# Rotary embedding of queries and keys cut into eight steps and spread over the attention heads, with the weight granules paired and ordered anew

## The chip, the cores and the metric

The kernel runs as one program on one core of a Trainium2 chip. The metric is device time in microseconds from the program's start to its end. Engine names are those of the profile: PE is TensorE's matrix multiply, PEld its weight load, DVE is VectorE, ACT is ScalarE, POOL is GpSimd, SP is SyncE, which issues most DMAs.

## What is computed

One layer of a flow-matching trunk on 640 tokens (512 latent tokens and 128 prompt tokens), width 1024, all in float32: a gated feed-forward half step, a mixing stage, and a second half step. The mixing stage runs eight heads of differential attention beside four heads of an mLSTM memory. The part that the change touches is the head of the attention:

```python
dq = rmsnorm(dq.reshape(B, T, DA_HEADS, 2, DA_HEAD_DIM), p['g_qn'][l])
dk = rmsnorm(dk.reshape(B, T, DA_HEADS, 2, DA_HEAD_DIM), p['g_kn'][l])
...
q_att = rope_2d(dq)
keys = jnp.concatenate([rope_2d(dk), k_ctx.astype(dk.dtype)], axis=1)
...
s = jnp.einsum('bqhcd,bkhcd->bhcqk', qi, kf) * scale
pr = jax.nn.softmax(s, axis=-1)
w = pr[:, :, 0] - lam * pr[:, :, 1]
return jnp.einsum('bhqk,bkhv->bqhv', w, vf)
```

Queries and keys are normalised per group of 64 numbers and then rotated by position ("rope"); prompt tokens are scaled only. Products are made from float32 numbers split into a high and a low part (H and L in the names), three matmuls for each product.

## The kernel before

Matmuls are written in a fixed order by hand (`mm`, L75, and the transposes, L78). On the other engines a scheduler places an instruction where it thinks best, unless it is issued inside `written()`: then instructions of one engine keep the order in which the code issues them.

**The attention** is the loop over eight heads and, within a head, five query blocks (qi 0 to 3 see 768 keys, qi 4 is the prompt block with 128). For one block: `scores` (eight matmuls into a three-bank PSUM tile `sc` of which there is one, then on DVE `mn`, L1674, the row minimum), `soft` (two exponentials on ACT, `p<-sc,mn`), `mix` (on DVE `rc`, `r` and the sum `p<-p,r,p`, L57), and, in the next block's place on PE, `turn` (transposes `ps_wT<-ident,p`) and `values` (`ps_o<-v_tok,wT`, evicted by DVE as `ao`, L61). At a head's end `finish_norm` normalises `ao` on DVE and ACT, and `finish` transposes it (`ps_aT<-ident,ao`) early in the next head. The next head's queries and keys are split by `pack` at qi 3 and transposed (`ps_qkT`) at the head's end.

**Fill units.** Between these steps PE is given other work from a queue, `Fill`: products of weight granules with the tokens, in units. A narrow token granule (`token`, 256 columns) has 5 units of 24 matmuls; two granules taken together (`wide`, 512 columns, in a PSUM bank of their own, `wide_ps`) have 10 units of 12 matmuls; a `feature` granule has 4 units of 24. The table `UNITS` says how many units stand in each block: a pair (1, 1) is two, (1, 0) is one. A granule's weights are split on ACT (`wH`) and DVE (`wL`, 2048 numbers per partition). Keys and queries of head pair `pr` (two heads) come from `project_k(pr)` and `project_q(pr)`, values from `project_v(pr)`; `memory_values`, `queries_of_memory` and `keys_of_memory` serve the later memory stage. In one unit order, 102 units are queued, the same ones before and after the change.

**The rotation.** When the last unit of a query or key granule is evicted by ACT, `qk_norm_rope` is issued at once, outside `written()`: a square on ACT (`rope<-k_tok`, 1280 numbers per partition), a sum on DVE (`ss`), a reciprocal root of 20 numbers (Ln and Exp on ACT, Newton on DVE, names `rv`, `rt`, `ry`), the scaling of 1280 numbers, a swapped copy on ACT (`rope<-k_tok`, 1024 numbers), and four more passes on DVE (times sine, times cosine, sum, prompt block times its gain). The scheduler sets these among the other DVE work. For a wide pair of keys and queries both rotations start with the same unit.

**PSUM pools.** Before the attention, a pool of five banks (`ps2`) serves the gate products, whose last results are evicted as `g_out` (the tile `ps_f`). It is closed, and two pools take over its banks in the order of their opening: `ps2m` (four banks, tag "mm", for all small tiles and narrow units) and `ps2w` (one bank, for wide units). A new tile waits until what last stood in its bank is evicted.

Of the kernel before, what the change touches and what calls it, by code (L numbers as in the profile page):

```python
# [31 lines left out]
def tile_trunk(ctx: ExitStack, tc: tile.TileContext, a: dict):  # L32
# [1494 lines left out]

    at_rope = [None]

    def qk_norm_rope(raw, tab):  # L1530
        A, B, g = tab
        sq = rope_place("q")
        act(sq, raw, AF.Square)
        ss = rope_p[0].tile([128, 20], F32, tag="ss", name="ss", bufs=2)
        vec.tensor_reduce(out=ss, in_=sq.rearrange("p t (g d) -> p (t g) d", d=64), axis=AX.X, op=ALU.add)
        rs = rstd_of(rope_p[0], ss, 1.0 / 64, [128, 20], "qk")
        r3 = raw.rearrange("p t (g d) -> p (t g) d", d=64)
        tt(vec, r3, r3, rs[:, :, None].to_broadcast([128, 20, 64]), ALU.mult)
        sw = rope_place("k")[:, 0:4]
        at_rope[0] = act(  # L1540
            sw.rearrange("p t (b s j) -> p (t b) s j", s=2, j=16),
            raw[:, 0:4, :].rearrange("p t (b s j) -> p (t b) s j", s=2, j=16)[:, :, ::-1, :],
            AF.Copy,
        )
        s4 = sw.rearrange("p t (g d) -> p t g d", d=64)
        q4 = raw[:, 0:4, :].rearrange("p t (g d) -> p t g d", d=64)
        tt(vec, s4, s4, B[:, :, None, :].to_broadcast([128, 4, 4, 64]), ALU.mult)
        tt(vec, q4, q4, A[:, :, None, :].to_broadcast([128, 4, 4, 64]), ALU.mult)
        tt(vec, raw[:, 0:4, :], raw[:, 0:4, :], sw, ALU.add)
        p3 = raw[:, 4, :].rearrange("p (g d) -> p g d", d=64)  # L1550
        tt(vec, p3, p3, g[:, None, :].to_broadcast([128, 4, 64]), ALU.mult)

    q_tok, k_tok, v_tok = {}, {}, {}

    def project_q(pr, now=lambda f: f()):
        def make():
            q_tok[pr] = t = (ap if pr % 2 else qk).tile([128, 5, 256], F32, tag="qtok", name="q_tok")

            def evac(p, i):
                act(t[:, i, :], p, AF.Copy)  # L1560
                if i == 4:
                    now(lambda: qk_norm_rope(t, tabs[0]))

            return evac

        return a["w_dq"][pr], make

    def project_k(pr, now=lambda f: f()):
        def make():
            t = (ap if pr % 2 else qk).tile([128, 5, 256], F32, tag="ktok", name="k_tok")  # L1570
            k_tok[pr] = t

            def evac(p, i):
                act(t[:, i, :], p, AF.Copy)
                def whole():
                    qk_norm_rope(t, tabs[1])
                    nc.sync.dma_start(out=a["new_k"][:, pr * 256 : (pr + 1) * 256], in_=t[:, 4, :])

                if i == 4:
                    now(whole)  # L1580

            return evac

        return a["w_dk"][pr], make
# [237 lines left out]
    token(project_v(0))  # L1822
    token(project_k(1))
    token(project_q(1))
    wide(project_v(1), memory_values(0))
    projections(2)
    queries_of_memory(1)
    wide(project_v(2), memory_values(1))
    projections(3)
    wide(project_v(3), memory_values(2))  # L1830
    keys_of_memory(1)
    queries_of_memory(2)
    keys_of_memory(2)
    queries_of_memory(3)
    values_of(3)
    feature(a["w_mk"][3], last_keys)
    gate_unit(a["w_gm"], gm_dram, 3, memory)
    gate_unit(a["w_gd"], gd_dram, 3, memory)
# [157 lines left out]
    ada.close()  # L1996
    right.close()
    banks.close()
    psum = att.enter_context(tc.tile_pool(name="ps2m", bufs=4, space=PSUM, reuse_waits="tile"))
    wide_ps.append(att.enter_context(tc.tile_pool(name="ps2w", bufs=1, space=PSUM, reuse_waits="tile")))  # L2000
    ap = att.enter_context(tc.tile_pool(name="att", bufs=1, reuse_waits="tile"))
    rope_p[0] = ap
    gt = gates.enter_context(tc.tile_pool(name="gates", bufs=1))
# [30 lines left out]
    late = None  # L2034
    for hd in range(8):
        H = heads[hd]
        for qi in range(5):
            n = UNITS[hd][qi]
            with written():
                H.scores(qi)  # L2040
                if qi > 0:
                    H.turn(qi - 1)
                H.soft(qi)
            aside(hd, qi, 0)
            fill.units(n[0])
            with written():
                H.mix(qi)
            if late is not None:
                late()
                late = None  # L2050
            if qi > 0:
                with written():
                    H.values(qi - 1)
            if qi == 3 and hd < 7:
                with written():
                    heads[hd + 1].pack()
            aside(hd, qi, 1)
            if (hd, qi) == (0, 2):
                begin_pools()
            fill.units(n[1])  # L2060
            with written():
                fill.ahead()
        n = UNITS[hd][-1]
# [571 lines left out]
```

## Time and profile before

| | |
|---|---|
| three runs | 1815.42, 1811.67, 1814.11 us; median 1814.11 |
| the profiled execution | 1810.32 us, of which the span from first to last instruction is 1808.4 |
| PE, PEld, DVE, ACT busy | 98%, 95%, 74%, 50% of the span |
| granted TensorE clock | 1.0 of full speed |
| attention stage | from about 650 us (first fill unit) to about 1065 us of the span |

The page of the profile gives busy shares; the view by windows gives the busy time of every engine in a stretch; the view of waits names for each idle time of an engine the instruction that ended it; the timeline gives start, duration and, in brackets, the idle time before an instruction. A share of the page is an average over stages with different limits, so the stage of the change is read by itself. In the groups view the last columns are busy time in us and the mean of one instruction in ns.

### The profile page before, as it was taken

Reading aid. Unit: us, or ns where it says so; the run is one execution under the profiler, and the core shown is the slowest. Engines: PE = TensorE matmul, PEld = TensorE weight load, DVE = VectorE, ACT = ScalarE, POOL = GpSimd, SP = SyncE. Lnnn points to the kernel's source line nnn. Section 1 sums busy time; section 2 is a strip of 40 time slices with the busy share of each in tenths; the row PEclk is TensorE's granted clock in tenths of the full one; section 3 lists DMA queues with packets and bytes.
Section 4 is the critical chain, followed back from the end, with each engine's and each line's share of the span. In section 5 each row is a group of like instructions: output and inputs, shape, how many; then the busy total and the mean of one; then the engine's idle time right before and its main releaser. Section 6 shows DMA issues by size and latency. Waiting matters only on the chain.

```text
span 1808.4 us, 29656 instructions
## 1 busy us (share of the span) xinstructions
PE 1778.9 (98%) x11950; PEld 1713.3 (95%) x11950; DVE 1346.6 (74%) x2162; ACT 900.2 (50%) x1579; POOL 41.0 (2%) x72
## 2 busy tenths in 40 slices
PE   8999999999999999999999999999999999999998
PEld 7999999999999999898889998899999999999998
DVE  6889987677988768667586447877668888897475
ACT  5654544333655456554565447562326545554432
POOL 0000000100000000000000000000000000000010
PEclk9999999999999999999999999999999999999999
DMA  8355566978245533312223335665652455557992
GB/s 325 114 198 173 185 236 220 351 223 272 84 138 183 195 129 100 110 61 69 75 72 110 106 99 197 188 244 205 217 173 77 134 173 187 203 180 272 355 311 84
DMA packets 144923, 317.85 MB, mean 176 GB/s; under 512 B 10577, under 2 KB 106577, under 8 KB 133009
## 3 DMA queue, kind: packets, MB, share of 16 engines
q1 hardware_dynamic: 133410, 270.20, 43.9%
q0 software_dynamic: 10688, 43.13, 7.4%
q10 hardware_dynamic: 688, 2.63, 0.4%
q8 instruction: 94, 1.54, 0.3%
q14 instruction: 43, 0.35, 0.1%
HBM read 243.77 MB, written 72.15 MB: 175 GB/s over the span
## 4 chain that ended last, share of the span: by engine, by line
PE 84%; DVE 8%; DMA 5%; ACT 2%; issue 1%; SPq 0%; DVEq 0%; ACTq 0%
PE ps_f L75 48%; PE ps_p L75 14%; PE ps_t L75 11%; PE sc L75 3%; PE ps_o L75 2%; PE ps_n L75 2%; DVE ww L54 2%; DMA raw_a<-in_w_ada_k 1%; PE ps_wT L78 1%; DMA P<-nm_dram 1%; PE ps_u L75 1%; PE ps_qkT L78 1%; DVE junk L814 1%; DMA raw<-in_w2b 1%; DMA a_raw<-aT_dram 1%
## 5 line engine op out<-in xcount | busy, mean ns | idle before, releaser
L75 PE MATMUL ps_f<-S,ww 128*128 128x320 f32 x2400 | 387.0, 309 | 3.2 <-DMA S<-g_dram 1.0
L75 PEld LDWEIGHTS ps_f<-S,ww 128*128 128x128 f32 x2400 | 359.8, 188 | 7.2 <-DVE ww L54 4.6
L54 DVE TENSOR_TENSOR ww<-raw,ww 128x2048 fp32r<-128x2048 f32 (+1 forms) x73 | 163.9, 2245 | 65.5 <-ACT ww L51 65.4
L75 PE MATMUL ps_f<-hm,ww 128*128 128x320 f32 x1176 | 185.6, 309 | 0.1
L75 PEld LDWEIGHTS ps_f<-hm,ww 128*128 128x128 f32 x1176 | 175.7, 188 | 0.3 <-DVE ww L54 0.3
L51 ACT ACTIVATE ww<-raw 128x2048 fp32r<-128x2048 f32 (+1 forms) x73 | 136.8, 1875 | 57.1 <-DVE raw L54 37.8
L54 DVE TENSOR_TENSOR raw<-raw 128x1024 f32<-128x1024 f32 x186 | 160.7, 864 | 2.4
L75 PE MATMUL ps_f<-hm,wB 128*128 128x320 f32 x1008 | 161.5, 309 | 0.0
L75 PE MATMUL ps_t<-wH,hH 128*128 128x256 f32 (+1 forms) x440 | 151.4, 344 | 2.9 <-DVE g_out L54 1.5
L75 PE MATMUL ps_p<-hH,wH 128*128 128x320 f32 x480 | 151.1, 315 | 1.6 <-DVE num L54 1.4
L75 PEld LDWEIGHTS ps_f<-hm,wB 128*128 128x128 f32 x1008 | 151.3, 188 | 0.0
L75 PE MATMUL ps_p<-hH,wL 128*128 128x320 f32 x480 | 148.3, 309 | 0.0
L75 PE MATMUL ps_p<-hL,wH 128*128 128x320 f32 x480 | 148.3, 309 | 0.0
L75 PE MATMUL ps_t<-wH,hL 128*128 128x256 f32 (+1 forms) x440 | 146.7, 333 | 0.9 <-DVE hL L54 0.9
L75 PE MATMUL ps_t<-wL,hH 128*128 128x256 f32 (+1 forms) x440 | 146.2, 332 | 0.0
L51 ACT ACTIVATE u<-ps_f 128x320 f32<-128x320 f32 x129 | 55.8, 433 | 157.0 <-PE ps_f L75 156.9
L51 ACT ACTIVATE wH<-raw 128x2048 fp32r<-128x2048 f32 (+1 forms) x45 | 75.4, 1683 | 48.8 <-PE ps_p L75 37.3
L54 DVE TENSOR_TENSOR wL<-raw,wH 128x2048 fp32r<-128x2048 f32 x37 | 84.6, 2286 | 19.5 <-ACT wH L51 19.3
L1674 DVE TENSOR_REDUCE mn<-sc 128x2 f32<-128x1536 f32 (+1 forms) x40 | 59.6, 1490 | 50.2 <-PE sc L75 50.0
L54 DVE TENSOR_TENSOR wB<-raw,wB 128x1024 fp32r<-128x1024 f32 x64 | 78.0, 1219 | 24.4 <-ACT wB L51 24.4
L814 DVE CUSTOM_DVE_ANT_0 junk<-raw_a,csil 128x1024 bf16<-128x1024 f32 (+1 forms) x76 | 92.5, 1217 | 2.1 <-DMA raw_a<-in_w_ada_c 1.6
L75 PEld LDWEIGHTS ps_t<-wH,hH 128*128 128x128 f32 x440 | 83.6, 190 | 11.0 <-DVE g_out L54 1.7
(306 smaller groups left out, 3595.9 us busy)
## 6 DMA issues: line engine op xcount, KB each, us to landing
g_dram<-g SPq DMA_DIRECT2D x44, 640.0 KB, 7.6
raw_a<-in_w_ada_c POOLq DMA_DIRECT2D x38, 512.0 KB, 5.1
g_dram<-g SPq DMA_DIRECT2D x24, 480.0 KB, 8.4
raw<-in_w1b SPq DMA_DIRECT2D x11, 1024.0 KB, 5.0
raw<-in_w3b SPq DMA_DIRECT2D x11, 1024.0 KB, 6.2
raw<-in_w1a SPq DMA_DIRECT2D x10, 1024.0 KB, 5.0
raw<-in_w3a SPq DMA_DIRECT2D x10, 1024.0 KB, 6.2
hm<-g_dram SPq DMA_DIRECT2D x7, 1280.0 KB, 11.8
```

Source lines behind the costliest of these rows:

```text
L51: return placed(nc.scalar.activation(*args, **kw))
L54: return placed(eng.tensor_tensor(out=out, in0=in0, in1=in1, op=op))
L75: tc.keep_in_program_order(nc.tensor.matmul(*args, **kw))
L78: tc.keep_in_program_order(nc.tensor.transpose(*args, **kw))
L814: placed(vec.tensor_tensor_reduce(out=junk, in0=raw, in1=self.csil[:, v, :], op0=ALU.mult, op1=ALU.add, scale=1.0, scalar=0.0, accum_out=m ...
L1674: placed(vec.tensor_reduce(out=mn, in_=sv, axis=AX.X, op=ALU.min))
```

## The change

1. `qk_norm_rope` becomes a list of eight steps (`rope_steps`): square, sums, root, divide, swap, by_sine, by_cosine, add. For the first head pair, which is projected before the attention, all eight still run at once. For the other three pairs the list is put on a queue, `rotations`, and a new function `rotate` issues one step (at some points of a pair of rotations two, one of the keys and one of the queries) inside `written()`. `rotate` is called up to three times per block, and not beside the prompt block's (qi 4) first place, nor at qi 3's second; beside a block with one unit its first call is left out when a `wL` split stands there. Before an odd head packs the next head, what is left on the queue is issued.
2. The order of granules: `project_v(1)` becomes a narrow granule, and `memory_values` 0 to 3 are paired with other partners, so that `memory_values(3)` is no longer a narrow granule near the end. `queries_of_memory(1)` moves from between the pairs to behind them. Narrow granules stay four, wide pairs five.
3. The pool of the wide bank, `ps2w`, opens ahead of `ps2m`.

```diff
-    def qk_norm_rope(raw, tab):
+    def rope_steps(raw, tab, then=lambda: None):
...
+        def square():
+            box["sq"] = rope_place("q")
+            act(box["sq"], raw, AF.Square)
+        def sums():
...
+        return [square, sums, root, divide, swap, by_sine, by_cosine, add]
+    def qk_norm_rope(*args):
+        for f in rope_steps(*args):
+            f()
+    rotations = []
+    def rotate():
+        if not rotations:
+            return False
+        first, second = rotations[0], rotations[1] if len(rotations) > 1 else []
+        had, left = len(first), len(second)
+        with written():
+            if had == 4 and left == 7 or had == 2 and left == 5:
+                second.pop(0)()
+            else:
+                first.pop(0)()
+                if (had, left) in ((5, 8), (4, 6)):
+                    second.pop(0)()
+            if not first:
+                rotations.pop(0)
+        return True
...
-                    now(lambda: qk_norm_rope(t, tabs[0]))
+                    if now:
+                        now(lambda: qk_norm_rope(t, tabs[0]))
+                    else:
+                        rotations.append(rope_steps(t, tabs[0]))
...
     token(project_q(1))
-    wide(project_v(1), memory_values(0))
+    token(project_v(1))
     projections(2)
+    wide(project_v(2), memory_values(0))
+    projections(3)
+    wide(project_v(3), memory_values(1))
+    wide(memory_values(2), memory_values(3))
     queries_of_memory(1)
-    wide(project_v(2), memory_values(1))
-    projections(3)
-    wide(project_v(3), memory_values(2))
     keys_of_memory(1)
     queries_of_memory(2)
     keys_of_memory(2)
     queries_of_memory(3)
-    values_of(3)
...
+    wide_ps.append(att.enter_context(tc.tile_pool(name="ps2w", bufs=1, space=PSUM, reuse_waits="tile")))
     psum = att.enter_context(tc.tile_pool(name="ps2m", bufs=4, space=PSUM, reuse_waits="tile"))
-    wide_ps.append(att.enter_context(tc.tile_pool(name="ps2w", bufs=1, space=PSUM, reuse_waits="tile")))
...
-                fill.low()
+                split = fill.low()
+            if qi < 4 and (UNITS[hd][qi][1] or not split):
+                rotate()
+        elif qi != 3:
+            rotate()
...
             if qi == 3 and hd < 7:
+                while odd and rotate():
+                    pass
...
             fill.units(n[1])
+            if n[1]:
+                rotate()
```

**DVE, prompt block of head 2.** `mn<-sc` here is the row minimum of the prompt block, `k_tok` and `rope` belong to the rotation of the keys of heads 4 and 5, `p_...` is the mixed softmax that PE's next transposes wait for, `ss` begins the rotation of the queries. Before:

```order
L1674 TENSOR_REDUCE mn<-sc 128x2
L54 TENSOR_TENSOR kL<-ck,kH 128x2x256
L54 TENSOR_TENSOR k_tok<-k_tok,g_kn 128x256
L54 TENSOR_TENSOR rope<-rope,ropeBk 128x1024
L54 TENSOR_TENSOR k_tok<-k_tok,ropeAk 128x1024
L1688 RECIPROCAL rc<-sm 128x2
L54 TENSOR_TENSOR k_tok<-k_tok,rope 128x1024
L57 SCALAR_TENSOR_TENSOR r<-sm,nlam,rc 128x1
L57 SCALAR_TENSOR_TENSOR p_8430<-p_8431,r,p_8430 128x128
L61 TENSOR_SCALAR ao<-ps_o,rc 128x128
L1535 TENSOR_REDUCE ss<-rope 128x20
L54 TENSOR_TENSOR kp_8498<-k_tok,kpk 128x10x64 x2
```

Now, at the same place:

```order
L1728 TENSOR_REDUCE mn<-sc 128x2
L54 TENSOR_TENSOR kL<-ck,kH 128x2x256
L1742 RECIPROCAL rc<-sm 128x2
L57 SCALAR_TENSOR_TENSOR r<-sm,nlam,rc 128x1
L57 SCALAR_TENSOR_TENSOR p_8444<-p_8445,r,p_8444 128x128
L61 TENSOR_SCALAR ao<-ps_o,rc 128x128
L54 TENSOR_TENSOR k_tok<-k_tok,ropeAk 128x1024
L54 TENSOR_TENSOR kp_8501<-k_tok,kpk 128x10x64 x2
```

Four passes of the rotation stood between the minimum and the mixed softmax, and the sum of the other rotation ahead of `kp`; now none stands ahead of the softmax, and one, behind it, ahead of `kp`.

**DVE, end of head 4 and start of head 5.** `ass`, `rv`, `rt`, `ry` and `ao<-ao,ry` are the normalisation of the finished head, for which PE's `ps_aT` waits; rows with 128x20 and `k_tok` are the rotation of the keys of heads 6 and 7. Before:

```order
L1720 TENSOR_REDUCE ass<-asq 128x5
L63 TENSOR_SCALAR rv<-ss 128x20
L63 TENSOR_SCALAR rv<-ass 128x5
L57 SCALAR_TENSOR_TENSOR rt<-ry 128x20
L57 SCALAR_TENSOR_TENSOR rt<-ry 128x5
L1674 TENSOR_REDUCE mn<-sc 128x2
L54 TENSOR_TENSOR rt<-rt,rv 128x20
L54 TENSOR_TENSOR rt<-rt,rv 128x5
L57 SCALAR_TENSOR_TENSOR ry<-rt,ry 128x20
L57 SCALAR_TENSOR_TENSOR ry<-rt,ry 128x5
L54 TENSOR_TENSOR k_tok<-k_tok,ry 128x1280
L54 TENSOR_TENSOR ao<-ao,ry 128x640
```

Now:

```order
L1774 TENSOR_REDUCE ass<-asq 128x5
L63 TENSOR_SCALAR rv<-ass 128x5
L57 SCALAR_TENSOR_TENSOR rt<-ry 128x5
L54 TENSOR_TENSOR rt<-rt,rv 128x5
L57 SCALAR_TENSOR_TENSOR ry<-rt,ry 128x5
L54 TENSOR_TENSOR ao<-ao,ry 128x640
L54 TENSOR_TENSOR wL<-raw,wH 128x2048
L1728 TENSOR_REDUCE mn<-sc 128x2
```

The rotation's small steps, its pass of 1280 numbers and the next head's first minimum stood inside the normalisation; now the normalisation stands ahead of the weight split and of that minimum, with nothing of the rotation in it.

**PE, first fill unit of the attention.** `ps_f` is the last gate product, `ps_t` the first unit's tile; the waits are in brackets. Before:

```order
L75 MATMUL ps_f_6516<-hH_4471,ww_6447 128x320
L75 MATMUL ps_f_6516<-hL_4472,ww_6447 128x320
L75 MATMUL ps_f_6516<-hH_4471,ww_6448 128x320
L75 MATMUL ps_t_6689<-wH_6606,hH_4471 128x256 [waits DVE_49]
L75 MATMUL ps_t_6689<-wL_6607,hH_4471 128x256
```

Now:

```order
L75 MATMUL ps_f_6516<-hH_4471,ww_6447 128x320
L75 MATMUL ps_f_6516<-hL_4472,ww_6447 128x320
L75 MATMUL ps_f_6516<-hH_4471,ww_6448 128x320
L75 MATMUL ps_t_6689<-wH_6606,hH_4471 128x256
L75 MATMUL ps_t_6689<-wL_6607,hH_4471 128x256 [waits DVE_49]
```

The first matmul no longer waits for DVE; the second one does, for the low part of its weights.

More of the change, by code (lines that the diff above doesn't have):

```diff
@@ L1528, in tile_trunk @@
     at_rope = [None]
-    def qk_norm_rope(raw, tab):
+    def rope_steps(raw, tab, then=lambda: None):
         A, B, g = tab
[L1532 to L1551, printed above, removed]
@@ new lines, in rope_steps @@
+        box = {}
+        def square():
+            box["sq"] = rope_place("q")
+            act(box["sq"], raw, AF.Square)
+        def sums():
+            box["v"], box["t"], box["y"], ss = (
+                rope_p[0].tile([128, 20], F32, tag="qk" + n, name="qk" + n, bufs=2) for n in ("v", "t", "y", "ss")
+            )
+            placed(vec.tensor_reduce(out=ss, in_=box.pop("sq").rearrange("p t (g d) -> p (t g) d", d=64), axis=AX.X, op=ALU.add))
+            ts(box["v"], ss, 1.0 / 64, ALU.mult, EPS, ALU.add)
@@ new lines, in root, with divide, swap @@
+        def root():
+            act(box["t"], box["v"], AF.Ln)
+            act(box["y"], box["t"], AF.Exp, scale=-0.5)
+        def divide():
+            newton_rsqrt(box["y"], box["v"], box["t"])
+            r3 = raw.rearrange("p t (g d) -> p (t g) d", d=64)
+            tt(vec, r3, r3, box["y"][:, :, None].to_broadcast([128, 20, 64]), ALU.mult)
+        def swap():
+            box["sw"] = rope_place("k")[:, 0:4]
+            at_rope[0] = act(
+                box["sw"].rearrange("p t (b s j) -> p (t b) s j", s=2, j=16),
+                raw[:, 0:4, :].rearrange("p t (b s j) -> p (t b) s j", s=2, j=16)[:, :, ::-1, :],
+                AF.Copy,
+            )
@@ new lines, in by_sine, with by_cosine, add @@
+        def by_sine():
+            s4 = box["sw"].rearrange("p t (g d) -> p t g d", d=64)
+            tt(vec, s4, s4, B[:, :, None, :].to_broadcast([128, 4, 4, 64]), ALU.mult)
+        def by_cosine():
+            q4 = raw[:, 0:4, :].rearrange("p t (g d) -> p t g d", d=64)
+            tt(vec, q4, q4, A[:, :, None, :].to_broadcast([128, 4, 4, 64]), ALU.mult)
+        def add():
+            tt(vec, raw[:, 0:4, :], raw[:, 0:4, :], box["sw"], ALU.add)
+            p3 = raw[:, 4, :].rearrange("p (g d) -> p g d", d=64)
+            tt(vec, p3, p3, g[:, None, :].to_broadcast([128, 4, 64]), ALU.mult)
+            then()
@@ L1553, in tile_trunk, with project_q @@
     q_tok, k_tok, v_tok = {}, {}, {}
-    def project_q(pr, now=lambda f: f()):
+    def project_q(pr, now=None):
         def make():
@@ L1561, in evac, with project_k @@
                 if i == 4:
-                    now(lambda: qk_norm_rope(t, tabs[0]))
+                    if now:
+                        now(lambda: qk_norm_rope(t, tabs[0]))
+                    else:
+                        rotations.append(rope_steps(t, tabs[0]))
             return evac
         return a["w_dq"][pr], make
-    def project_k(pr, now=lambda f: f()):
+    def project_k(pr, now=None):
         def make():
@@ L1574, in evac, with store @@
                 act(t[:, i, :], p, AF.Copy)
-                def whole():
-                    qk_norm_rope(t, tabs[1])
+                def store():
                     nc.sync.dma_start(out=a["new_k"][:, pr * 256 : (pr + 1) * 256], in_=t[:, 4, :])
                 if i == 4:
-                    now(whole)
+                    if now:
+                        now(lambda: qk_norm_rope(t, tabs[1], store))
+                    else:
+                        rotations.append(rope_steps(t, tabs[1], store))
             return evac
@@ L2036, in tile_trunk @@
         H = heads[hd]
+        odd = hd % 2
         for qi in range(5):
```

## The prediction

> **What bounds the kernel now.** I read the page first, then the view by windows over the attention stage, then PE's waits there, then the timeline around each.
>
> ```profile
> span 1808.4 us, 29656 instructions
> PE 1778.9 (98%) x11950; PEld 1713.3 (95%) x11950; DVE 1346.6 (74%) x2162; ACT 900.2 (50%) x1579; POOL 41.0 (2%) x72
> ```
>
> PE has work in 98% of the span, and the change leaves every matmul in place, so it can only win idle time of PE. By windows (length, then busy time of PE, PEld, DVE, ACT, POOL, then the granted clock):
>
> ```profile
> 640.00:660.00 20.00, 18.52 (x135) 18.26 (x134) 9.93 (x14) 11.70 (x17) 0.00 (x0) 1.00 0.61 206
> 660.00:700.00 40.00, 39.56 (x332) 38.95 (x332) 30.68 (x50) 21.56 (x42) 0.00 (x0) 1.00 0.34 94
> 700.00:760.00 60.00, 60.00 (x374) 52.89 (x374) 44.19 (x66) 36.42 (x72) 0.00 (x0) 1.00 0.28 91
> 760.00:800.00 40.00, 40.00 (x239) 34.67 (x237) 23.91 (x38) 23.04 (x52) 0.00 (x0) 1.00 0.18 58
> 800.00:840.00 40.00, 36.51 (x246) 33.65 (x246) 35.19 (x55) 25.40 (x52) 0.00 (x0) 1.00 0.34 103
> 920.00:960.00 40.00, 38.27 (x214) 32.27 (x213) 33.97 (x54) 24.56 (x57) 0.00 (x0) 1.00 0.20 71
> ```
>
> In most of the stage PE is full and DVE has room (23.91 of 40 us in 760 to 800). In two stretches, 800 to 840 and 920 to 960, DVE is at 34 to 35 of 40 and PE loses 3.49 and 1.73 us; at 640 to 660 it loses 1.48. All of PE's waits from 640 to 1065 (total, times, longest):
>
> ```profile
> PE ps_wT L78 <- DVE p L57: 2.2, 3, 1.8
> PE ps_aT L78 <- DVE ao L54: 2.1, 2, 1.7
> PE ps_t L75 <- DVE g_out L54: 1.5, 1, 1.5
> PE ps_qkT L78 <- DVE ao L61: 1.2, 1, 1.2
> PE ps_o L75 <- ACT wT L51: 0.5, 1, 0.5
> PE ps_t L75 <- DVE kH L1650: 0.4, 1, 0.4
> PE ps_p L75 <- ACT kL L51: 0.2, 1, 0.2
> ```
>
> That is 8.1 us, 0.45% of the span, and the ceiling of what the stage can give. Where the large ones lie (start, duration, idle time before):
>
> ```profile
> 654.68 0.39 PE L75 MATMUL ps_t<-wH,hH 128*128 128x256 f32 x1 [1.48 <-DVE g_out L54]
> 819.59 0.30 PE L78 MATMUL ps_wT<-ident,p 128*128 128x128 f32 x1 [1.83 <-DVE p L57]
> 826.36 0.37 PE L78 MATMUL ps_qkT<-identr,kpk 128*128 128x128 f32 x2 [1.21 <-DVE ao L61]
> 837.74 0.77 PE L78 MATMUL ps_aT<-ident,ao 128*128 128x128 f32 x5 [0.46 <-DVE ao L54]
> 931.24 0.77 PE L78 MATMUL ps_aT<-ident,ao 128*128 128x128 f32 x5 [1.68 <-DVE ao L54]
> ```
>
> **The change part by part.** *Rotations.* What DVE and ACT did ahead of the wait at 819.59:
>
> ```profile
> 815.11 0.20 ACT L51 ACTIVATION_READ_ACCUMULATOR p<-sc,mn 128x1 f32 x1
> 815.32 1.22 DVE L54 TENSOR_TENSOR rope<-rope,ropeBk 128x1024 f32<-128x1024 f32 x1
> 816.45 1.22 DVE L54 TENSOR_TENSOR k_tok<-k_tok,ropeAk 128x1024 f32<-128x1024 f32 x1
> 817.59 0.16 DVE L1688 RECIPROCAL rc<-sm 128x2 f32<-128x2 f32 x1
> 817.71 1.22 DVE L54 TENSOR_TENSOR k_tok<-k_tok,rope 128x1024 f32<-128x1024 f32 x1
> 819.10 0.35 DVE L57 SCALAR_TENSOR_TENSOR p<-p,r,p 128x128 f32<-128x128 f32 x1
> ```
>
> The exponentials were done at 815.31, and the reciprocal came 2.3 us later, behind passes of the rotation; a third pass stands between it and `p`. The waits at 826.36, 837.74 and 931.24 have the same neighbours: the second rotation, then `ao` behind the first rotation's 1280-number pass. One rotation costs DVE, by the groups in this stage (count, busy, mean ns):
>
> ```profile
> L1535 DVE TENSOR_REDUCE ss<-rope 128x20 f32<-128x1280 f32 x6 | 8.9, 1482 | 2.2 <-ACT rope L51 2.2
> L54 DVE TENSOR_TENSOR k_tok<-k_tok,ry 128x1280 f32<-128x1280 f32 x3 | 4.5, 1490 | 0.0
> L54 DVE TENSOR_TENSOR rope<-rope,ropeBk 128x1024 f32<-128x1024 f32 x3 | 3.7, 1221 | 0.2 <-ACT rope L51 0.2
> L54 DVE TENSOR_TENSOR wL<-raw,wH 128x2048 fp32r<-128x2048 f32 x20 | 45.7, 2285 | 7.1 <-ACT wH L51 6.8
> ```
>
> 1.48 for the sum, 1.49, three passes of 1.22, and some 1.1 for the prompt block's pass and the small ones: 7.7 us. For a pair 15.5 us, which now fall within about one head and in the change within some eight blocks of two heads. The work is the same; only its place changes. In the row order none of the four places has a rotation's pass ahead of what PE waits for, so I take all four away: 1.83 + 1.21 + 0.46 + 1.68 = 5.18 us (bounds: 5.2 if nothing is late next, 2.6 if half is).
>
> What is late next: in a block with one fill unit the chain from the scores to `p` is the tightest. In head 2 it ran so:
>
> ```profile
> 805.85 0.40 PE L75 MATMUL sc<-kL,qT 128*128 128x512 f32 x1
> 806.28 1.76 DVE L1674 TENSOR_REDUCE mn<-sc 128x2 f32<-128x1536 f32 x1 [0.77 <-PE sc L75]
> 807.96 2.28 DVE L54 TENSOR_TENSOR wL<-raw,wH 128x2048 fp32r<-128x2048 f32 x1
> 810.71 1.02 DVE L57 SCALAR_TENSOR_TENSOR p<-p,r,p 128x768 f32<-128x768 f32 x1
> ```
>
> `p` is ready 5.9 us after the last score, and the gap between minimum and reciprocal holds one `wL` of 2.28 us. In the change such a gap holds a rotation's scaling instead (three small instructions and 1.49, about 2.0 us), which fits, but PE comes sooner: units at that place are now 512 wide. In the chain that ended last, a narrow unit, the scores of two blocks of which the first has one unit, a wide unit and a feature unit:
>
> ```profile
> 693.39 2.88 PE ps_t L75 x24
> ...
> 789.02 1.39 PE sc L75 x8
> ...
> 795.16 1.40 PE sc L75 x8
> ...
> 843.33 2.75 PE ps_t L75 x12
> ...
> 1003.54 3.52 PE ps_p L75 x24
> ```
>
> The unit between those scores and the transposes took 3.52 and now takes 2.75, so 0.8 us of cover is gone: I expect a wait of 0.2 to 0.6 us at qi 3 of heads 2 and 4. Second, in qi 1 of these heads DVE has minimum 1.68, split 2.2, `rc`, `r`, `p` 1.5, `ao` 0.3 and the scaling 2.0, some 7.8 us with its starts, in a block in which PE needs 6.1 (795.16 less 789.02 above); that makes the next minimum 1.7 us late, and the next block has a second unit, 2.75 more, to cover it. Head 0's prompt block, with a split and a sum in its row, has some tenths of slack. I price new waits at 1.3 us (bounds 0 and 3: six rotations of 0.5 each).
>
> *PSUM order.* The wait at 654.68 is for the bank under the first unit's tile. With the wide bank opened first, that tile moves to another bank, whose result was evicted earlier, and the last bank goes to the wide pool, which is first used some twenty units on. The second matmul's wait is for the low weights, split at
>
> ```profile
> 644.48 2.29 DVE L54 TENSOR_TENSOR wL<-raw,wH 128x2048 fp32r<-128x2048 f32 x1 [5.22 <-ACT wH L51]
> ```
>
> thus done at 646.8. Everything behind starts 1.48 us sooner, and DVE and ACT there wait for PE (DVE is at 9.93 of 20), so I keep 1.4 (bounds 0.5, if a bank of another unit is late instead, and 1.5).
>
> *Granules.* The same 20 narrow units, 50 wide and 32 feature units are run, so PE's work is unchanged, and so is the number of splits. At the end of head 7, feature units of 3.52 stand where narrow ones of 2.88 stood; 0.2 us of cover more at one of the last waits, against a split that moves into the prompt block: nothing. In the memory stage's first 30 us loads and evictions come in a little different order; I take 0, with bounds of 1 us either way, the size of one of the waits listed above.
>
> [...]
>
> Sum: -5.2 - 1.4 + 1.3 = -5.3 us. The profiled execution took 1810.32 us (1808.4 of span, 1.9 around it) and would take 1805.0; it lies 3.8 under the median of 1814.11, and I apply the same difference to the median: **1808.8 us**, 0.29% less. About 0.2%, 3.6 us, is what a measurement of this kernel can tell from no change (its three runs span 3.75 us).
>
> **The rivals.** *The waits only move.* The steps are fixed in a row, and a block with one unit has no room; half of the 5.2 comes back as small waits in six rotations. For it: the 7.8 us against 6.1 above. Against it: over 660 to 800 DVE is busy 99 of 140 us. Then -2.6 - 1.4 + 1.3 = -2.7: 1811.4, no change that can be told.
>
> *Slower: DVE stands in line behind ACT.* A rotation has three hand-overs from ACT to DVE (square to sum, root to Newton, swap to sine). In a fixed row DVE waits there with the next minimum and `p` queued behind it, and PE waits for `p`. The row of `ss` above has 2.2 us of waiting for ACT in six. If each of the 18 hand-overs costs PE 0.6 us, that is 10.8 against 6.6 won: +4.2, 1818.3. It cancels the gain from 0.37 us each. Against it: square and swap are issued a step ahead of their readers, and ACT is about half busy.
>
> *Much faster: PE's busy time hides waits.* In 700 to 760 PEld is busy 52.89 of 60 us. If the missing 7.1 us were waiting and all came back over 660 to 1050, that would be 46 us: 1768. Against it: 12 wide matmuls take 2.75 us in the chain, 0.229 each, with no idle time between, so a load is shorter than the matmul that covers it. [...]
>
> **How the numbers follow.** Forecast 0.67, moving waits 0.24, slower 0.08, much faster 0.01. The likeliest case's own range: at best all of 5.2 + 1.5, 0.9 of small waits and 1 in the memory stage, -8.6; at worst 5.2 + 0.5 won and 3 + 1 lost, -1.7: 1805.5 to 1812.4. With 1 us for the median of few runs, and the case of moving waits inside it: 1804.5 to 1813. Faster by over 0.2%: 0.67 + 0.01 = 0.68. Within 0.2%: 0.24. Slower: 0.08.
>
> **What would show it.** Right: in PE's waits of the stage `ps_t <- g_out` gone, `ps_wT <- p`, `ps_aT <- ao` and `ps_qkT <- ao` below 1.5 us in sum against 5.5, DVE's busy share level between the heads, and PE's busy time the same. Wrong: a wait of PE for `p` in blocks with one unit of heads 2 and 4 above 0.6 each; DVE waiting for ACT `rope` ahead of `mn`; an attention stage shorter by the amount forecast but a memory stage longer.

## The result and the profile after

The changed kernel took 1819.43 us (median of six runs, 1817.05 to 1822.12), the kernel before 1812.6 beside it (six runs, 1811.67 to 1815.42): a ratio of 1.0035, 95% interval 1.0022 to 1.0048. It is slower by some 7 us, where 5.3 us less was forecast, and the time lies outside the range. The same kernel was run once more with the last experiments: 1819.12 against 1810.8, ratio 1.0045 (1.0033 to 1.0058). One run of the kernel before, beside the first experiments, took 1920.89 us at a granted clock of 0.851 and is in no ratio here.

The profiled execution's span is 1818.7 us. From the page, PE's share is what it was:

```profile
span 1818.7 us, 29656 instructions
PE 1784.0 (98%) x11950; PEld 1715.6 (94%) x11950; DVE 1348.7 (74%) x2162; ACT 899.6 (49%) x1579; POOL 40.8 (2%) x72
```

PE's waits of the changed kernel from 640 to 1065 us (total, times, longest), to be held against the seven rows of before:

```profile
PE ps_t L75 <- ACT stage L51: 5.2, 3, 2.1
PE ps_t L75 <- ACT q_tok L51: 2.0, 2, 1.0
PE ps_qkT L78 <- ACT v_tok L51: 1.2, 1, 1.2
PE ps_o L75 <- ACT wT L51: 0.5, 1, 0.5
PE ps_t L75 <- DVE kH L1704: 0.4, 1, 0.4
```

The rows `ps_t <- g_out`, `ps_wT <- p`, `ps_aT <- ao` and `ps_qkT <- ao` are gone from this stretch, as forecast. One wait for `p` stays: the one at head 7's prompt block, 0.21 us before, is 0.71 now and lies just behind the stretch, at 1065.22. In place of the others stand 7.2 us of fill units (`ps_t`) that wait for ACT to evict `stage` (the buffer from which results of the memory are stored) or `q_tok`, and 1.2 us for `v_tok`. The waits are 9.3 us in all, 10.0 with the one at head 7, against 8.1. The windows of the changed kernel (columns as before) show the loss at other places:

```profile
640.00:660.00 20.00, 20.00 (x147) 20.00 (x146) 10.64 (x14) 11.17 (x16) 0.00 (x0) 1.00 0.62 203
660.00:700.00 40.00, 38.43 (x321) 37.64 (x320) 31.22 (x53) 22.76 (x44) 0.00 (x0) 1.00 0.32 91
...
760.00:800.00 40.00, 37.89 (x212) 32.19 (x211) 21.19 (x35) 22.25 (x48) 0.00 (x0) 0.96 0.18 58
800.00:840.00 40.00, 39.37 (x234) 33.74 (x232) 31.90 (x51) 23.84 (x55) 0.00 (x0) 1.00 0.21 65
```

In 800 to 840 PE lost 3.49 us before and loses 0.63 now, with DVE down from 35.19 to 31.90; but 760 to 800, which was full, loses 2.11, and its clock reads 0.96. The first 20 us are full now, and the next 40 lose 1.57 where they lost 0.44.

**Where the largest new wait comes from.** The timeline of the changed kernel at the first block of head 2 (ACT's rows, and PE's next matmul of a fill unit):

```profile
788.27 0.90 ACT L51 ACTIVATE p<-sc,mn 128x768 f32<-128x768 f32 x1 [4.72 <-DVE mn L1728]
...
789.16 0.89 ACT L51 ACTIVATE p<-sc,mn 128x768 f32<-128x768 f32 x1
...
790.03 1.27 ACT L51 ACTIVATE rope<-k_tok 128x1280 f32<-128x1280 f32 x1
791.19 0.38 ACT L51 ACTIVATE v_tok<-ps_t 128x256 f32<-128x256 f32 x1
791.46 0.39 ACT L51 ACTIVATE stage<-ps_t 128x256 f32<-128x256 f32 x1
...
791.90 0.50 PE L75 MATMUL ps_t<-wH,hH 128*128 128x512 f32 x1 [2.11 <-ACT stage L51]
```

`v_tok<-ps_t` and `stage<-ps_t` empty a wide tile, which stands in the one bank of its pool. PE filled it with this block's first unit and wants the bank for the second; only five transposes (`ps_aT`) lie between. The two evictions stand on ACT behind the block's exponentials, which wait for the row minimum, and here also behind the rotation's square. The kernel before, at the same place:

```profile
781.63 0.39 ACT L51 ACTIVATE k_tok<-ps_t 128x256 f32<-128x256 f32 x1 [1.96 <-PE ps_t L75]
781.91 0.38 ACT L51 ACTIVATE q_tok<-ps_t 128x256 f32<-128x256 f32 x1
784.81 0.90 ACT L51 ACTIVATE p<-sc,mn 128x768 f32<-128x768 f32 x1 [2.52 <-DVE mn L1674]
```

There the tile was closed by the last unit of head 1, and evicted 3 us ahead of the exponentials. A wide tile takes two units, so what counts is whether a head begins on an odd or an even one. By the queue's order, counted from 0, the wide units begin with unit 15 before (three narrow granules of five) and with unit 20 now (four), the feature granule between the pairs has an even number, and heads 1 to 5 begin with units 21, 31, 41, 51 and 61. So the first unit of a head opened a tile before, and closes one now.

**The memory stage** is the second place. The stage begins with the transposes `ps_k`; the difference of the marks that the timelines give for its start and for the first product of its attended part (`aHL`) is 128.39 us before, 131.41 after. Its products `ps_n` need the tile `P`, which is loaded from memory and first passes DVE. DVE's first pass over `P`, before and after (one fence each):

```profile
1083.33 0.82 DVE L54 TENSOR_TENSOR P<-P,mask 128x640 f32<-128x640 f32 x1 [4.65 <-DMA P<-nm_dram]
```

```profile
1094.25 0.82 DVE L54 TENSOR_TENSOR P<-P,mask 128x640 f32<-128x640 f32 x1 [20.75 <-DMA P<-nm_dram]
```

`ps_k` begins at 1084.03 before and 1090.79 after, so `P` came 0.7 us ahead of it and now comes 3.5 us behind. PE waits for it in the changed kernel, where the longest wait for `P` before was 0.2 us:

```profile
PE ps_n L75 <- DVE P L54: 2.8, 1, 2.8
```

The loads of `P` are issued on SP. First the kernel before (the keys `mkT` are out at 1028 and 1034, and `P` follows at 1075.87), then the changed one (three of the keys' 640 KB loads come just ahead of `P`), then what those loads waited for in the changed kernel:

```profile
1028.07 0.80 SPq L1772 DMA_DIRECT2D mkT<-mk_dram  x2
1034.47 0.32 SPq L1772 DMA_DIRECT2D mkT<-mk_dram  x1
...
1075.87 1.03 SPq L97 DMA_DIRECT2D P<-nm_dram  x2
```

```profile
1079.88 0.80 SPq L1826 DMA_DIRECT2D mkT<-mk_dram  x2
1081.20 0.73 SPq L1826 DMA_DIRECT2D mkT<-mk_dram  x1
...
1083.75 1.40 SPq L97 DMA_DIRECT2D P<-nm_dram  x2
```

```profile
SPq L1826 <- PE ps_p L75: 2.7, 1, 2.7
```

They waited for a feature unit of PE: the memory under the keys was still held by weights.

### The profile page after: what moved, and what is told of

It reads as the page before. It is cut to its first block, busy times and chain, and to the rows that moved or that the text cites. A ratio compares the mean times of both kernels' runs of the same rounds, so it can differ in the third digit from the quotient of the medians.

```text
span 1818.7 us, 29656 instructions
## 1 busy us (share of the span) xinstructions
PE 1784.0 (98%) x11950; PEld 1715.6 (94%) x11950; DVE 1348.7 (74%) x2162; ACT 899.6 (49%) x1579; POOL 40.8 (2%) x72
## 4 chain that ended last, share of the span: by engine, by line
PE 80%; DVE 9%; DMA 6%; ACT 3%; issue 1%; SPq 0%; DVEq 0%; ACTq 0%
PE ps_f L75 46%; PE ps_p L75 14%; PE ps_t L75 10%; PE sc L75 3%; PE ps_o L75 2%; DVE ww L54 2%; DMA raw<-in_w2b 2%; PE ps_n L75 1%; DMA raw_a<-in_w_ada_k 1%; DMA P<-nm_dram 1%; PE ps_wT L78 1%; PE ps_qkT L78 1%; DVE mn L1728 1%; DVE junk L814 1%; PE ps_u L75 1%
```

## The experiments

Theory *Bank*: the shifted places and the one wide bank cost the time, and what ACT holds ahead of the evictions sets how much. Rivals: *Hand-overs*, the slower case of the prediction (the rotation's fixed steps make DVE stand behind ACT), and *Memory stage* (other loads and another order there). The kernels ran in three groups, each beside runs of the kernel before, whose median was 1809.84, 1809.77 and 1810.8 us (1812.6 beside the first runs of the changed kernel); so differences to it are compared and not times.

| kernel | minus before, us | ratio (95%) | attention | memory | low-clock stretches, attention and memory |
|---|---|---|---|---|---|
| before | 0 | 1 | 429.35 | 128.39 | 0, 0 |
| changed, first profile | +6.8 | 1.0035 (1.0022 to 1.0048) | 435.96 | 131.41 | 2, 0 |
| e11 changed again | +8.3 | 1.0045 (1.0033 to 1.0058) | 432.66 | 133.12 | 0, 2 |
| e1 before, new order only | +15.2 | 1.0083 (1.0069 to 1.0097) | 438.82 | 133.48 | 2, 1 |
| e2 before, new pools only | +0.2 | 1.0004 (0.9995 to 1.0012) | 432.17 | 127.65 | 2, 0 |
| e8 before, shifted | +4.2 | 1.0027 (1.0017 to 1.0037) | 434.47 | 127.44 | 0, 0 |
| e14 before, new order, shifted | -2.2 | 0.9988 (0.9979 to 0.9997) | 427.38 | 127.09 | 0, 0 |
| e3 changed, shifted | -3.5 | 0.9984 (0.9975 to 0.9993) | 428.51 | 126.76 | 0, 0 |
| e10 e3, all first steps late | -5.1 | 0.9972 (0.9962 to 0.9982) | 426.01 | 126.48 | 0, 0 |
| e13 e10, gate rows late | -4.9 | 0.9973 (0.9962 to 0.9983) | 427.38 | 126.74 | 0, 0 |
| e12 changed, evictions first | +2.8 | 1.0018 (1.0009 to 1.0028) | 430.71 | 131.01 | 0, 1 |
| e5 changed, step behind the unit | +9.2 | 1.0066 (1.0044 to 1.0088) | 435.09 | 133.73 | 1, 2 |
| e9 changed, spare slot closed earlier | +3.9 | 1.0021 (1.0010 to 1.0032) | 434.51 | 126.54 | 1, 0 |
| e4 changed, two wide banks | +20.5 | 1.0110 (1.0095 to 1.0124) | 446.97 | 132.52 | 5, 1 |

"Attention" runs in one profile from the start of the first fill unit to `ps_k`; up to there each kernel has run the same 90 units. "Memory" runs from `ps_k` to the first matmul with `aHL`. With the old pools, the wait for `g_out` (1.1 to 1.5 us) lies just ahead of the first mark. The last column counts stretches of about 3.4 us in which the granted TensorE clock is at half, in the one profile of each kernel; the last section shows one. In the attention one of them cost 1.5 us where the same place was also profiled at the full clock (11.36 against 9.87 us, last section).

**e1, the order alone.** The kernel before with the new block of granules:

```diff
-    wide(project_v(1), memory_values(0))
+    token(project_v(1))
     projections(2)
...
-    values_of(3)
```

> The kernel before with only the new order of granules; rotations at once and pools as before. Theory Bank: with four narrow granules first instead of three, the wide granules' half units change places against the heads, so that the first unit of each head closes a tile and the second needs its one bank again while ACT holds the evictions behind the block's exponentials; five such places at about 1.2 us each, so 4 to 8 us slower than before, with waits of PE ps_t for ACT stage or v_tok at the first block of heads 1 to 5. Theory Hand-overs (the rotation's steps in a fixed row make DVE stand behind ACT): the rotations aren't changed here, so within 1.5 us of before. Theory Memory stage (other loads and another order there): 1 to 3 us slower, all of it after the attention.

It was 15.2 us slower, nearly twice the most that Bank said, and slower than the whole change. So the order is the part that loses, and the rotations' steps don't lose but win against it. Bank's size was short for two reasons: the waits were longer than 1.2 us,

```profile
PE ps_t L75 <- ACT stage L51: 5.4, 3, 2.8
PE ps_t L75 <- ACT q_tok L51: 3.3, 2, 2.8
```

8.7 us in sum, with two low-clock stretches; and the memory stage is 5.1 us longer, with one low-clock stretch in it, which only Memory stage had said. Both have a share.

**e2, the pools alone.**

```diff
+    wide_ps.append(att.enter_context(tc.tile_pool(name="ps2w", ...
     psum = att.enter_context(tc.tile_pool(name="ps2m", bufs=4, ...
-    wide_ps.append(att.enter_context(tc.tile_pool(name="ps2w", ...
```

> The kernel before with only the wide bank's pool opened first. What I put on record: the wait of 1.5 us on g_out goes, 1.4 us faster. Theory Bank (the bank that is late is only another one): the wait on g_out goes, and one of about 1.2 us on ACT's eviction v_tok comes some 9 us later, at the first head's queries; 0 to 0.5 us faster. Hand-overs and Memory stage say nothing of it.

No difference: the first unit starts at 653.20 and not 654.68, and this row is new, some 10 us later:

```profile
PE ps_qkT L78 <- ACT v_tok L51: 1.7, 1, 1.7
```

On ACT the evictions of the first units stand there behind four bias rows and three passes of the memory's gates (`ig`, `fg`, `e`), which run from 659.18 to 663.94 with one eviction between them. The bank that I thought was free early is another unit's, and it is late as well. Bank's forecast holds.

**e3, shifted.** The changed kernel with one more unit at the end of head 0; from head 1 on, the first unit of a head opens a tile again.

```diff
-    UNITS[0] = (two, two, two, two, one, (1, 1, 1))
+    UNITS[0] = (two, two, two, two, one, (2, 1, 1))
```

> The changed kernel with one unit more at the end of head 0 (2, 1, 1), so that from head 1 on the first unit of a head opens a tile again, as before the change; all else as changed. Theory Bank: the five waits for ACT stage and q_tok at the first blocks of heads 1 to 5 go, 8.3 us of PE's excess there, and with them the 3.3 us that the lower clock cost at heads 2 and 4: 8 to 11 us faster than the changed kernel, about 4 us faster than before. Theory Hand-overs: DVE still stands in line behind ACT, 0 to 1 us faster than changed. Theory Memory stage: 0 to 1 us.

3.5 us faster than before, and 11.8 below the changed kernel by their differences to before (-3.5 and +8.3; 10.3 by -3.5 and +6.8). The size fits Bank, but its working fits only in part: of that the attention has only 4.2 (428.51 against e11's 432.66). The 7.2 us of waits at the first blocks went, and two others came:

```profile
PE ps_t L75 <- ACT stage L51: 2.7, 2, 1.4
PE ps_qkT L78 <- ACT v_tok L51: 1.6, 1, 1.6
```

The other 6.4 us are in the memory stage, which I had given 0 to 1. Against the first profile of the changed kernel it is 7.5 and 4.7, since the half clock fell in the attention there and in the memory stage in e11. The shift had changed more than the places: by the rule that hands out the places for split weights, worked through for each order, the spare slot holds the last queries of the memory (`queries_of_memory(3)`) in the changed kernel, and in e3 `queries_of_memory(2)`, which ends two granules earlier. The loads of the keys, into memory that the slot's pool had held, came at 1027.04 and 1050.94 in e3.

**e9, the spare slot alone.** The changed kernel with this slot closed to the last queries; the attention's places as changed.

```diff
-        if self.spare is not None and "x" not in self.live and i + 3 < len(self.q):
+        if self.spare is not None and "x" not in self.live and i + 4 < len(self.q):
```

> The changed kernel with the spare slot of weights closed to one granule more (the condition i + 4 in place of i + 3), so that the last queries of the memory don't lie in it and the memory stage's loads of keys needn't wait for their last unit; the attention as changed. Theory Memory stage, second cause beside Bank: PE's wait of 2.8 us for P at the start of the memory stage goes and the stage's start is 3 us shorter, 3 to 5 us faster than the changed kernel, with the waits in the attention as they are. Theory Bank alone: within 1 us of the changed kernel. Theory Hand-overs: no change.

4.4 us below the changed kernel (+3.9 against +8.3; 2.9 against +6.8): the keys' loads start at 1014.92, 1019.55 and 1060.67, `P`'s at 1080.86,

```profile
1060.67 0.32 SPq L1826 DMA_DIRECT2D mkT<-mk_dram  x1
...
1080.86 1.04 SPq L97 DMA_DIRECT2D P<-nm_dram  x2
```

`ps_n` no longer waits for `P`, and the memory stage takes 126.54 us, as in e3. That is 4.9 less than in the first profile of the changed kernel (131.41); in neither of the two does the clock fall in this stage. Against e11 (133.12), where it does, it is 6.6. The waits for `stage` and `q_tok` are the same 7.2 us. So the memory stage is a cause by itself. (The attention is 1.9 us longer than e11's by one low-clock stretch, 1.5 us.)

**e8, the places alone.** The kernel before with the edit of e3: nothing of the change, but the first unit of heads 1 to 5 now closes a tile.

> The kernel before with one unit more at the end of head 0 and nothing else: rotations at once, granules and pools in their old order, but the first unit of heads 1 to 5 now closes a wide tile, as it does in the changed kernel. Theory Bank: waits for ACT stage, k_tok, q_tok or v_tok at those first blocks, 5 to 9 us slower than before, all of it in the attention (the memory stage's loads of keys come as early as before). Theory Hand-overs and theory Memory stage: within 1 us of before.

4.2 us slower, with the memory stage at 127.44. PE waits before the second unit of each of the five heads, 0.97, 1.02, 1.02, 1.02 and 1.22 us; the first of them:

```profile
744.14 0.50 PE L75 MATMUL ps_t<-wH,hH 128*128 128x512 f32 x1 [0.97 <-ACT stage L51]
```

Bank alone, then, without a step of a rotation in the kernel, costs about 1 us a head, 5.3 in the five. The other two theories said 1 us at most. The whole kernel lost less, because the shift moved the rotations against the blocks too: the waits for `ao` of before are gone here and those for `p` are 3.3 us and not 2.2, so all waits behind the first fill unit grew by 4.0.

**e5 and e12, the square behind the evictions.** Both mean to take the rotation's step at a head's first block out of the evictions' way; e5 by issuing it behind the unit,

```diff
-            if qi < 4 and (UNITS[hd][qi][1] or not split):
+            if 0 < qi < 4 and (UNITS[hd][qi][1] or not split):
...
             fill.units(n[0])
+            if qi == 0:
+                rotate()
```

> The changed kernel with the rotation's step at the first block of a head issued behind that block's first unit, so that at heads 2 and 4 the square stands behind ACT's evictions of that unit and not ahead of them; order and places of units as changed. Theory Bank: the waits there fall from 2.1 us to about 1 us, and the clock no longer falls behind them (1.7 us each): 4 to 6 us faster than the changed kernel, so 1 to 3 us slower than before; the other waits at first blocks (heads 1, 3, 5) and the memory stage stay. Theory Hand-overs (the steps make DVE stand behind ACT): a step later on ACT comes later to DVE, 0 to 2 us slower than changed. Theory Memory stage: no change.

e5 was 9.2 us slower than before, no better than the changed kernel. The edit did not do what it says. The evictions aren't issued in `written()`, and the scheduler set them behind the step all the same. At heads 2 and 4 ACT's order is that of the changed kernel, and the wait is 2.11 us again; at head 1 the swapped copy, which stood behind the evictions, now stands ahead:

```profile
739.54 1.05 ACT L51 ACTIVATE rope<-q_tok 128x1024 f32<-128x1024 f32 x1
740.49 0.38 ACT L51 ACTIVATE k_tok<-ps_t 128x256 f32<-128x256 f32 x1
740.75 0.39 ACT L51 ACTIVATE q_tok<-ps_t 128x256 f32<-128x256 f32 x1
741.19 0.50 PE L75 MATMUL ps_t<-wH,hH 128*128 128x512 f32 x1 [1.96 <-ACT q_tok L51]
```

It raised that wait from 1.02 to 1.96. So e5 tells about the mechanism, and nothing about its own question. e12 holds the step back by a dependence:

```diff
...
-            if qi < 4 and (UNITS[hd][qi][1] or not split):
+            if 0 < qi < 4 and (UNITS[hd][qi][1] or not split):
...
+            if qi == 0:
+                with tc.issue_after(evicted[0].ins):
+                    rotate()
```

> The changed kernel with the rotation's step at the first block of a head held back until ACT has evicted that block's first unit, so that the square at heads 2 and 4 really stands behind the evictions; places of units, pools and order as changed. Theory Bank: the two waits of 2.1 us there fall to about 1.0 each, 2.2 us faster than the changed kernel, and up to 3 us more where the clock no longer falls behind them (1.45 us each time): 2 to 5 us faster than changed. The three waits of about 1 us at heads 1, 3 and 5 stay. Theory Hand-overs: 0 to 1 us slower than changed.

2.8 us slower than before, 5.5 below the changed kernel. Now the evictions stand ahead, and the wait at head 2 is 0.95:

```profile
787.69 0.38 ACT L51 ACTIVATE v_tok<-ps_t 128x256 f32<-128x256 f32 x1
787.96 0.39 ACT L51 ACTIVATE stage<-ps_t 128x256 f32<-128x256 f32 x1
788.22 1.29 ACT L51 ACTIVATE rope<-k_tok 128x1280 f32<-128x1280 f32 x1
```

All five waits are now 0.95 to 1.01, 4.9 us in sum. Against e11's profile the attention is 1.95 us shorter. The memory stage is 2.1 shorter too, where PE waited 2.3 us for `P` and not 3.5, and the profile has one low-clock stretch in place of two; that wait varies between profiles of kernels with the late keys (2.3 to 3.7), and Bank has no claim on it. Of the 5.5, then, Bank's share is 2 to 3.4, the last if a low-clock stretch, which most runs may have had, is counted.

Over e1, e5, e8, e11 and e12 the wait goes with what ACT does between the exponentials and the evictions: nothing, 0.95 to 1.2 us (0.55 once, in e1); the swapped copy (1.05), 1.96; the square (1.27), 2.11; a weight split `wH` (1.91), 2.35, 2.76 and 2.80. At e1's head 4 the evictions stand ahead of the exponentials, and the wait is 0.2. The split is what made e1's waits long:

```profile
790.24 1.91 ACT L51 ACTIVATE wH<-raw 128x2048 fp32r<-128x2048 f32 x1
...
792.31 0.39 ACT L51 ACTIVATE stage<-ps_t 128x256 f32<-128x256 f32 x1
```

**e4, two wide banks.** The changed kernel with two banks for wide units and three for small tiles.

```diff
-    ... tc.tile_pool(name="ps2w", bufs=1, ...
-    ... tc.tile_pool(name="ps2m", bufs=4, ...
+    ... tc.tile_pool(name="ps2w", bufs=2, ...
+    ... tc.tile_pool(name="ps2m", bufs=3, ...
```

> The changed kernel with two banks for wide units and three for the small tiles, in place of one and four. Theory Bank: the same waits go as by the shift, since the second tile of a head has a bank of its own; 8 to 11 us faster than changed, less what the narrow units and transposes lose with three banks (bounds 0 and 6 us, seen as waits of ps_aT, ps_wT or ps_qkT for evictions). Theory Hand-overs and theory Memory stage: no gain, and the same loss from three banks.

20.5 us slower than before: a bad trade, and worse than the bound that I gave. The waits of `ps_t` for `stage` and `q_tok` are gone, as Bank says, but three banks are too few for everything else, and behind the new waits the clock falls more often than in any other kernel here (five stretches in the attention, one in the memory stage):

```profile
PE ps_p L75 <- ACT stage L51: 3.6, 2, 1.8
PE ps_t L75 <- DVE kH L1704: 3.1, 1, 3.1
```

**e14, order and shift without steps.** The kernel before with the new order and the shift. It differs from e3 by the steps and the pools, and e2 prices the pools at nothing.

> The kernel before with the new order of granules and one unit more at the end of head 0: rotations at once and pools as before, but the first unit of a head opens a tile, and the memory's keys are loaded early. It differs from the changed and shifted kernel by the rotations' steps and the pools alone. My term for the rotations, 5.2 us: this is 4 to 6 us slower than the shifted kernel, so 1 to 3 us slower than before, with waits of PE for p and ao at heads 2 and 4 as before the change. Theory Hand-overs (steps lose what they win): within 1 us of the shifted kernel.

2.2 us faster than before, where 1 to 3 slower was expected: 1.3 from e3, with intervals that overlap. That is nearer to what Hand-overs had said (within 1 us of e3) than to my term of 5.2. The four waits of before, 5.2 us, are two here with no step at all, because the later granules set the rotations beside other blocks. The one for `p` and the one of `ps_qkT` are gone; `ps_aT` waits for `ao` at the start of heads 2 and 4, where it had waited 0.46 and 1.68 us at the start of heads 3 and 5:

```profile
PE ps_aT L78 <- DVE ao L54: 3.3, 2, 1.7
```

So in this order the steps can win 3.3 us, not 5.2. In e3 they give 2.7 of it back: ACT's swapped copy stands ahead of the evictions at the third blocks of heads 2 and 4. That was the row with `stage` above.

**e10, shifted, and all first steps late.** e3, with each block's first step issued behind its first unit.

```diff
...
-            if qi < 4 and (UNITS[hd][qi][1] or not split):
-                rotate()
+            step = qi < 4 and (UNITS[hd][qi][1] or not split)
...
+        return step
...
-            aside(hd, qi, 0)
+            step = aside(hd, qi, 0)
             fill.units(n[0])
+            if step:
+                rotate()
```

> The changed kernel shifted by one unit at the end of head 0, and with each first step of a block (not at the first blocks alone) issued behind the block's first unit. The shifted kernel still shows two waits of 1.4 us for ACT stage, at the third blocks of heads 2 and 4, where the rotation's swapped copy stands ahead of the evictions. Theory Bank: these two go as well, 2 to 3 us faster than the shifted kernel, so 5.5 to 6.5 us faster than before. Theory Hand-overs: steps that come later cost DVE, 0 to 2 us slower than the shifted kernel.

5.1 us faster than before, the best of all; the wait for `stage` is down from 2.7 to 0.6:

```profile
PE ps_t L75 <- ACT stage L51: 0.6, 2, 0.3
```

The attention is 2.5 us shorter than e3's. In the medians the step is 1.6, less than the 2 to 3 expected, and the intervals overlap.

**e13, the gate rows late.** e10, with the memory's gate rows held back on ACT until the first values are evicted.

```diff
...
-    with tc.issue_after(heads[0].at_vec.ins), tc.issue_after(heads[0].at_act.ins):
+    with tc.issue_after(heads[0].at_vec.ins), tc.issue_after(evicted[0, 4].ins):
...
```

> The shifted kernel with all first steps late, and with the memory's gate rows held back on ACT until the fifth unit of the first values is evicted. The evictions of the first three units then don't stand behind the gate rows' four bias rows and three passes, and PE's wait of 1.3 us for v_tok at the first head's queries should go: 1.3 us faster than the same kernel with the gate rows early, so about 6.3 us faster than before. That is the 1.4 us of the pools' order, if nothing else is late there; if the gate rows now delay the first head's keys or the first scores, 0 to 2 us slower than the kernel with the rows early.

No gain (4.9 against 5.1 faster than before). The wait for `v_tok` is gone, and two others are new at the first head's second block, 25 us later:

```profile
PE ps_wT L78 <- DVE p L57: 1.7, 2, 1.5
...
PE sc L75 <- ACT p L51: 0.9, 1, 0.9
```

The time that the pools' order sets free can be moved, but it was not kept in any kernel here.

**e11** is the changed kernel as the reference of the last group; its numbers stand above.

> The changed kernel itself, beside the other three, as their reference. All theories: 6 to 8 us slower than before, waits of PE for ACT stage and q_tok of about 7 us in the attention.

## Why the prediction was wrong

*Rotations, -5.2: right in what it took away, but not all the steps' doing, and not free.* All four waits went, and of the other waits for DVE only the one at head 7's prompt block grew, by 0.5 us; the prediction had put the end of head 7 at nothing. e14 shows that the order with a shift lowers the four from 5.2 to 3.3 us without any step. And the prediction asked what the steps do to DVE, while their squares also stand on ACT ahead of the evictions: that is 2.3 of the 7.2 us below (e12: 4.9).

*The step that failed: "Granules ... nothing", and 0 with a bound of 1 us for the memory stage.* PE's work is unchanged, as I said, and I took it that nothing else depends on the order. Two things do. The units' places decide which unit closes a wide tile, and with one bank that cost 7.2 us of new waits, 4.9 of them without the steps' squares (e8 brings such waits into the kernel before, e3 takes them out of the changed one). The granules' places decide which weights hold the spare slot last, and thus when the memory's keys can be loaded; e9 takes that away and wins 2.9 to 4.4 us. By the profiles the stage lost 3.0 us against before with the clock full, and 4.7 in e11 with the clock at half for 6.8 us of it.

*PSUM order, -1.4: failed.* The wait moved about 10 us on, to `ps_qkT` (e2: ratio 1.0004, 0.9995 to 1.0012). I had looked for the bank's last use before the attention, and not for the next tile that takes the bank in turn.

*New waits, +1.3: wrong place and engine.* They were to be waits for `p` at the fourth blocks of heads 2 and 4; the trace has none there. What PE waits for is evictions on ACT.

*The sum* closes on the second profile of the changed kernel, in which the clock stays full in the attention. Behind the first fill unit PE waits 9.9 us up to 1065, where it waited 6.6 (8.1 less the 1.48 of `g_out`): +3.3, and the attention is 3.3 longer (432.66 less 429.35). The memory stage adds 4.7. These 8.0 are the 7.9 by which the spans differ (1816.3 less 1808.4). In the memory stage of that profile the clock does fall; in the first profile it stays full there, and the stage adds 3.0. So where the clock is full the two stages lose 3.3 and 3.0, 6.3 us together.

*Rivals.* "The waits only move" was near in kind, yet they moved to ACT and not within DVE, and it priced too little. "DVE stands in line behind ACT" forecast a slower kernel, 1818.3, for a reason that the trace refutes: PE's waits for DVE up to 1065 us shrank from 7.4 to 0.4, DVE's own waits for ACT's `rope` up to 1072 us fell from 2.4 to 0.8, and e1, without any step, loses 15.2. That its time lies near the measured one is luck. The much faster case, with its 46 us from the time in which PEld isn't busy, fell too: PE's share stayed at 98% and PEld's at 94 to 95% in a kernel that got slower.

*What stays open.* How much of the 6.8 to 8.3 us the clock makes. By the 6.3 above it is an estimated 0.5 to 2.0 us more than the kernel before loses by it. The mean granted clock of every run is known: 0.996 to 0.998 in the eleven runs of the changed kernel, 0.996 to 1.0 and mostly 0.999 in 66 runs of the kernel before. In e9 the two runs at 1.0 took 1809.44 and 1810.49 us, and the three at 0.997 took 1814.81 to 1820.02, so the clock goes with several microseconds there; where it fell in a run without a profile is not known. Open is also how far the late `P` alone, without the keys' loads ahead of it in the queue, lengthens the stage. The kernel e10 is 0.28% faster than before, and part of that is the shift and not the change.

## What to carry to other kernels

When work units that share a buffer in pairs are put in a new order, count whether each stage begins on the first or the second unit of a pair, and look at what its evictions stand behind on their engine's queue: that decided the cost here, not the units' length. A place in memory handed out by a rule moves with the order too, so list who holds it last and which later load waits for it. A step that is spread out to free one engine should be followed on every engine that it issues to.

## What the runs showed of the hardware that was not expected

In these profiles, late in some of PE's waits or just behind them, the granted clock fell to half (0.50 in the windows inside such a stretch) for about 3.4 us. The changed kernel's first profile behind the wait of 2.11 us at 791.90, in windows of 2 us, and then its second profile at the same place (there from 791.25 on), where it stayed full:

```profile
790.00:792.00 2.00, 0.10 (x1) 0.10 (x1) 1.76 (x4) 2.00 (x6) 0.00 (x0) 1.00 0.00 0
792.00:794.00 2.00, 2.00 (x7) 1.63 (x8) 1.22 (x2) 1.36 (x5) 0.00 (x0) 0.76 0.42 155
794.00:796.00 2.00, 2.00 (x6) 1.51 (x6) 0.00 (x0) 1.56 (x1) 0.00 (x0) 0.50 0.26 89
796.00:798.00 2.00, 2.00 (x13) 1.68 (x12) 0.06 (x1) 0.00 (x0) 0.00 (x0) 0.89 0.39 121
```

```profile
791.40:793.40 2.00, 2.00 (x9) 1.65 (x10) 1.17 (x2) 1.36 (x5) 0.00 (x0) 1.00 0.43 163
793.40:795.40 2.00, 2.00 (x12) 1.73 (x11) 0.00 (x0) 1.52 (x1) 0.00 (x0) 1.00 0.22 82
```

In the first, the clocks of 0.76, 0.50 and 0.89 miss 1.7 us of full clock in sum, which is 3.4 us at half. A 512-wide matmul starts every 0.43 us there and not every 0.23. From the first scores of the head's first block to those of the second it took 11.36 and 9.87 us in the two: 1.5 for a stretch. The same wait of 2.1 us stands at heads 2 and 4 of the changed kernel (two profiles), e5 and e9; three of the eight were followed by half the clock. Of the other attention waits, it followed 1.73, 1.83 (e2), 1.96 (e5), 2.76 and 2.80 us (e1), and not 1.83 (before), 1.76 (e12) or 2.35 (e1). In e4 it came with 1.82 (twice), 2.22 and 3.11 us and not with 1.89. The wait for `P` in the memory stage has it too: with 2.27 (e12), 3.16 (e4), 3.21 (e1), 3.45 (e11) and 3.68 us (e5), and not with 2.81 (the first profile). In these profiles it came with no wait below 1.7 us, in neither stage. In e11 it lasts 6.8 us (four `ps_u` products take 1.93 us at 1097.18 and 1.03 at 1100.81), of which this is the second window:

```profile
1094.00:1096.00 2.00, 1.53 (x4) 1.28 (x5) 1.69 (x5) 2.00 (x7) 0.00 (x0) 0.50 1.02 416
```

So the length alone doesn't decide: behind the same wait of 2.1 us at head 2, one profile of the changed kernel has half the clock and the other the full one. What does decide, no run here shows; the shortest wait that it followed took 1.73 us.
